# A feed-forward block in seven products: partial products run k block after k block, weight sums and gate rows moved

## The chip, the cores and the metric

The kernel runs on one core of a Trainium2 chip. The engines it uses are TensorE (PE: matmuls, with PEld for the load of their stationary operand), VectorE (DVE), ScalarE (ACT), GpSimd (POOL) and SyncE (SP, which issues the DMAs). The metric is the time of one execution in device microseconds; the median of three runs is given for the kernel before.

## The reference

One layer of a decoder: a mixing sub-layer (pooling and dilated attention heads) and a gated feed-forward block with a short convolution, each between norms and with a residual. 1024 tokens, a model width of 1024, an inner width of 2816. The change touches the feed-forward block and the end of the norm before it:

```
h  = rms_norm(x, g_pre_ffn) * (1.0 + sc_f) + sh_f
up = h @ w_up                                   # 1024 x (2 * 2816)
gate, val = up[..., :D_FF], up[..., D_FF:]
gate = conv over 3 tokens(gate) + conv_b
y  = (gelu(gate) * val) @ w_down
x  = x + gt_f * rms_norm(y, g_post_ffn)         # gt_f: a row of c_act @ w_ada + b_ada
```

## The kernel before

**Precision.** Every float32 factor is split in a high part, which TensorE takes in its rounded format, and a low part, the remainder. A product a x w is three partial products: high x high, high x low, low x high. ScalarE copies the high part, VectorE subtracts to get the low part. In the code the weights' parts are `wh`, `wl`, the activations' `ah`, `al` (or `gh`, `gl` in the down projection).

**Up projection.** It goes in 22 chunks `c` of 128 inner columns (gate and value together). Each chunk is a 2 x 2 block product done with seven block products instead of eight, numbered 1 to 7. The token halves of h and their sums are the moving operands (`a11`, `a12`, `a21`, `a22` and the sums `s1` to `s4`), the four weight blocks b11, b21, b12, b22 and their sums `t1` to `t4` the stationary ones; `USES` (L1049) says which product takes which. A product (`product`, L1058) has four k blocks of 128 and so twelve matmuls of 128 x 128 on 128 x 512, all into one bank of PSUM: per k block wh x ah (L1066), wh x al (L1067), wl x ah (L1068). From the second chunk on, GpSimd makes the sums t1 to t4 (`total`, L1135), ScalarE their high parts (`prep`, L1139) and VectorE their low parts (`lower`, L1132). VectorE also takes the finished banks (`evac`, L1072, and `first`, L1038) and runs the convolution.

**The order of the work.** TensorE, ScalarE, VectorE and GpSimd run in the order in which the program writes their instructions; nothing passes on one engine. `steps` (L1190) is the list of products from the second chunk on. At step i the weights of up to six later steps are prepared (`prep_up`, L1296), due tasks are run (`run_tasks`), and then the product is issued. SyncE's DMAs are issued in order on a queue of their own.

**The first chunk** (L983 to L1115, and L1303 to L1310) is written out by hand, between the end of the norm and the steady state. `stats` (L877) scales the tiles of tokens; the last tile (7) is scaled by VectorE at L899. It stands in the program ahead of the split of the fourth chunk's up-weights (`up_load(3)`, L985). The transposed tokens come back through ScalarE (L914); `sums` (L936) makes s1 to s4 for the second token half (VectorE, L941), `parts` splits them (ScalarE L122, VectorE L169), `start_sum` (L949) makes t1 to t4 of the first chunk (VectorE, L951). Order around product 7: s4's split, product 3, then sum s3, sum t3, split of t3, split of s3, product 7, the reading of products 6 and 5. Sum t4 stands later, at L1306, behind the split of b22 (L1304) and the reading of product 3. GpSimd's first t2 sum, for the second chunk, writes the tile that t4 reads, so it comes after t4.

**The gate row.** gt_f is made beside the up projection, in two halves of 512 columns: eight rows per half, one load each (SyncE, 256 KB, L1207) into one buffer, then one accumulation on VectorE (L1209, L1211). One row is done per step, from 14 steps before product (5, c) on, c being 16 for the first half and 19 for the second (L1254 to L1258); at product (5, c) one matmul sums over the partitions (`gate_sum`, L1215).

**Down projection.** Again seven products, in the order 1, 2, 6, 5, 3, 7, 4, each with eleven k blocks. Four token blocks t have a bank each. `down` (L1356) issues, for one k block and one t, gh x wh (L1361), gh x wl (L1362), gl x wh (L1363); the loop at L1409 goes over k and in it over t. With the last k block the sum of a bank is taken out (`out_sum`). In the last product the k blocks from 5 on are run t by t.

Of the kernel before, what the change touches and what calls it, by code (L numbers as in the profile page):

```python
# [15 lines left out]
P = 128  # L16
# [72 lines left out]
MLAG = (20, 48)  # L89
SPACE = 3  # L90
AHEAD = 3
GATE_AT = 16
SKIP = (0, 1, 4)
ENDS = 6
LAG_LO, LAG_EV = 1, 1
# [8 lines left out]
def block_kernel(ctx: ExitStack, tc: tile.TileContext, x, pos, cols, rows, consts, w_ada_a, w_ada_b, w_in_u,  # L104
# [764 lines left out]
    if True:  # L869
# [7 lines left out]
        def stats(ys, xs):  # L877
            n = len(ys) + len(xs)
            q = ep.tile([P, 4], F32, name="q1", tag="q1", bufs=3)
            yv = {}  # L880
            for i, t in enumerate(ys):
                d = st8[t]
                yv[t] = PS[:, y_bank(t):y_bank(t) + 2, :].rearrange("p a b -> p (a b)")
                d["xr"] = ep.tile([P, D], F32, name="xr", tag="xr", bufs=6)
                nc.sync.dma_start(d["xr"], xv[:, t])
                d["x1"] = ep.tile([P, D], F32, name="x1", tag="x1", bufs=4)
                junk = ep.tile([P, D], F32, name="junk", tag="junk")
                nc.scalar.activation(junk, yv[t], AF.Square, accum_out=q[:, i:i + 1])
            for i, t in enumerate(xs, len(ys)):
                junk = ep.tile([P, D], F32, name="junk", tag="junk")  # L890
                nc.scalar.activation(junk, st8[t]["x1"], AF.Square, accum_out=q[:, i:i + 1])
            r = rsqrt(q[:, 0:n], root(q[:, 0:n], n), n)
            for i, t in enumerate(ys):
                d = st8[t]
                nc.vector.scalar_tensor_tensor(d["x1"], yv[t], r[:, i:i + 1], gtg, op0=ALU.mult, op1=ALU.mult)
                nc.vector.tensor_add(d["x1"], d["x1"], d["xr"])
                nc.sync.dma_start(x1v[:, t], d["x1"])
            for i, t in enumerate(xs, len(ys)):
                nc.vector.tensor_scalar_mul(st8[t]["xr"], st8[t]["x1"], r[:, i:i + 1])  # L899

        def x_turn(m, r):
            for i in range(4):
# [24 lines left out]
        def side(name, k):  # L927
            for k0, h, l in reversed(A[name]):
                if k >= k0:
                    return h[:, k - k0], l[:, k - k0]  # L930
# [14 lines left out]
        def new_piece():  # L945
            at["p"] += 1
            return ring[(at["p"] - 1) % len(ring)]
# [5 lines left out]
        def start_piece(n, src):  # L953
            W[n, 0] = new_piece()
            split(src, *W[n, 0])
# [11 lines left out]
        if True:  # L967
# [90 lines left out]
            def product(n, c):  # L1058
                a, w = USES[n]
                wh, wl = W.pop((w, c))  # L1060
                used[n, c] = idle.pop(0)
                o = bank(used[n, c])
                for k in range(4):
                    ks = slice(k * P, (k + 1) * P)
                    ah, al = side(a, k)
                    nc.tensor.matmul(o, wh[:, ks], ah, start=k == 0, stop=False)  # L1066
                    nc.tensor.matmul(o, wh[:, ks], al, start=False, stop=False)  # L1067
                    nc.tensor.matmul(o, wl[:, ks], ah, start=False, stop=k == 3)  # L1068

            lo, hi = slice(0, 512), slice(512, 1024)  # L1070

# [25 lines left out]
            pairs_of("s4")  # L1097
            parts("s4", all_t)
            product(3, 0)
            sums(hi_t, (3,))  # L1100
            start_sum("t3", b12, b12, b22)
            more = r1.tile(half, F32R, name="more", tag="rb2")
            ring[:] = [(more[:, 2 * i], more[:, 2 * i + 1]) for i in range(2)]
            at["p"] = 0
            start_piece("t3", b12)
            pairs_of("s3")
            parts("s3", all_t)
            gelu = cp.tile([P, 1], F32, name="gelu")
            nc.scalar.activation(gelu, one, AF.Gelu_apprx_tanh)
            product(7, 0)  # L1110
            evac(6, 0)
            A["22"] = [(0, *(r2.tile(half, F32R, name="b22", tag=t) for t in ("r2a", "r2b")))]
            s1g = cp.tile([P, 512], F32, name="s1g", tag="cst")
# [5 lines left out]
    if True:  # L1119
# [131 lines left out]
            if n in (3, 4, 6, 7):  # L1251
                at_step(now[0] + LAG_EV, lambda: (evac(n, c), finish_4(c) if n == 4 else None))

        for hf, c in ((0, GATE_AT), (1, GATE_AT + 3)):  # L1254
            i = steps.index((5, c))
            EXTRA.setdefault(i, []).append(lambda hf=hf, c=c: gate_sum(hf, c))
            for kb in range(8):
                EXTRA.setdefault(i - 14 + kb, []).append(lambda hf=hf, kb=kb: gate_acc(hf, kb))  # L1258
        for c in range(1, NC_FF - 1):
            EXTRA.setdefault(START_AT[c] + 5, []).append(lambda c=c: at_step(now[0], lambda: first(c + 1)))  # L1260

# [41 lines left out]
        prep_up(5, 5)  # L1303
        parts("22", all_t)  # L1304
        evac(3, 0)
        start_sum("t4", b21, b21, t2r)  # L1306
        more = r1.tile([P, 8, 512], F32R, name="more", tag="rb0")
        ring += [(p1[:, 0], p1[:, 1])] + [(more[:, 2 * i], more[:, 2 * i + 1]) for i in range(4)]
        prep_up(6, 6)
# [30 lines left out]
    with tc.manual_schedule(engines={ET.PE}):  # L1340
# [12 lines left out]
        def dbank(n, t):  # L1353
            return bank(idle[4 * (DOWN.index(n) % 2) + t])

        def down(n, t, ks):  # L1356
            o = dbank(n, t)
            ts_ = slice(t * P, (t + 1) * P)
            for k in ks:
                (gh, gl), (wh, wl) = DW[n, k]  # L1360
                nc.tensor.matmul(o, gh[:, ts_], wh, start=k == 0, stop=False)  # L1361
                nc.tensor.matmul(o, gh[:, ts_], wl, start=False, stop=False)  # L1362
                nc.tensor.matmul(o, gl[:, ts_], wh, start=False, stop=k == KD - 1)  # L1363

        def y_half(T, hf, y, z=None):
            sl = slice(hf * 512, (hf + 1) * 512)
# [42 lines left out]
        for i, (n, k) in enumerate(dq):  # L1409
            while ready < i + AHEAD_D:  # L1410
                prep_down(ready)
                ready += 1
            if n == DOWN[-1] and k > KD - ENDS:
                continue
            ks = range(k, KD) if n == DOWN[-1] and k == KD - ENDS else (k,)
            for t in range(4):
                down(n, t, ks)
                if ks[-1] == KD - 1:
                    out_sum(n, t)


def _host(inputs):
# [56 lines left out]
```

## Time and profile before

| | |
|---|---|
| median of 3 runs | 1072.24 us (1071.94 to 1073.34) |
| the profiled execution's own time | 1068.81 us |
| its span, first to last instruction | 1067.0 us |
| mean granted TensorE clock | 0.993 |
| TensorE busy | 1034.3 us, 97% of the span |
| VectorE busy | 849.4 us, 80% |
| ScalarE busy | 479.4 us, 45% |
| GpSimd busy | 223.3 us, 21% |
| first chunk by hand, from product 5 on | 438 to 464 us of the span |
| up projection, products on TensorE | 438 to 850 us |
| down projection | 850 to 1060 us |

All times in the views count from the first instruction of the span. A row of a timeline has the start, the length, engine, line, operation, written tile <- read tiles, shape, count, and in brackets the idle time of the engine before it and what ended that. A row of waits has the total, the number and the longest. A row of stretches has its bounds, its length, and for each of PE, PEld, DVE, ACT and POOL the busy time and (x) the instructions, then the granted TensorE clock, the DMAs' busy share and GB/s. Grouped rows have the busy time and the mean in ns. A matmul's length in a row is modelled and overlaps the next one's; the distance of two starts is the better measure.

### The profile page before, as it was taken

The page shows a single profiled execution, that of the slowest core. Times are in us where ns is not written, and L with a number is a line of the kernel's source. Part 1 is how long each engine was busy: PE and PEld are TensorE (multiplying, and loading weights), DVE is VectorE, ACT ScalarE, POOL GpSimd, SP SyncE. Part 2 cuts the span into 40 slices and gives each one's busy share as a digit, 9 for nine tenths or more (in the row PEclk, how much of TensorE's full clock was granted, in tenths as well). Part 3 has the DMA queues.
Part 4 walks back from the last instruction along what each step waited for, and adds up shares of the span by engine and source line. Part 5 has one row for each costly group of instructions (what it writes and reads, how often), then busy time and mean ns, then how long its engine had stood idle before and what let it go on. Part 6 is the DMA issues. An engine that isn't in the chain of part 4 may idle for free.

```text
span 1067.0 us, 15433 instructions
## 1 busy us (share of the span) xinstructions
PE 1034.3 (97%) x5174; PEld 875.2 (82%) x5174; DVE 849.4 (80%) x1840; ACT 479.4 (45%) x963; POOL 223.3 (21%) x132
## 2 busy tenths in 40 slices
PE   4999999999999999899999999999999999999997
PEld 4988988899888788678888888888878878888885
DVE  7975467885558778989998987979789999756898
ACT  6764342433354378633443433333233365544542
POOL 0000000000000000064333333324235525103460
PEclk9999999999999999999999999999999999999999
DMA  9652446362131164224434333344534879566563
GB/s 350 226 158 79 118 110 199 93 189 79 52 95 49 50 237 151 97 91 146 147 129 162 126 123 135 134 161 151 162 115 155 294 274 380 168 195 209 200 207 119
DMA packets 85148, 168.34 MB, mean 158 GB/s; under 512 B 9158, under 2 KB 25926, under 8 KB 81356
## 3 DMA queue, kind: packets, MB, share of 16 engines
q1 hardware_dynamic: 85068, 167.35, 47.3%
q8 instruction: 41, 0.67, 0.3%
q14 instruction: 39, 0.32, 0.1%
HBM read 134.47 MB, written 32.84 MB: 157 GB/s over the span
## 4 chain that ended last, share of the span: by engine, by line
PE 67%; DVE 17%; DMA 6%; issue 4%; ACT 4%; SPq 0%; DVEq 0%; POOL 0%; ACTq 0%; POOLq 0%
PE PS L1068 7%; PE PS L1067 7%; PE PS L1066 7%; PE PS L1362 6%; PE PS L1361 6%; PE PS L1363 6%; PE PS L220 5%; PE PS L222 4%; PE PS L221 4%; DMA gm<-in_w_ada_b_dram 3%; PE PS L709 3%; PE PS L679 2%; DVE more L1133 2%; PE PS L699 1%; DMA mraw<-in_w_ada_b_dram 1%
## 5 line engine op out<-in xcount | busy, mean ns | idle before, releaser
L1137 POOL TENSOR_TENSOR raws<-rw 128x512 f32<-128x512 f32 x30 | 48.2, 1606 | 495.6 <-DMA rw<-in_w_up_dram 438.1
L220 PE MATMUL PS<-wh,hh 128*128 128x384 f32 x336 | 124.6, 371 | 0.8 <-DVE vs L269 0.7
L222 PE MATMUL PS<-wh,hl 128*128 128x384 f32 x336 | 113.2, 337 | 0.0
L221 PE MATMUL PS<-wl,hh 128*128 128x384 f32 x336 | 112.9, 336 | 0.0
L122 ACT ACTIVATE more<-raws 128x512 fp32r<-128x512 f32 x79 | 48.2, 624 | 74.0 <-PE PS L1067 57.1
L220 PEld LDWEIGHTS PS<-wh,hh 128*128 128x128 f32 x336 | 63.4, 189 | 9.1 <-issue 4.8
L688 ACT ACTIVATE pm<-pm,nm 128x128 f32<-128x128 f32 (+1 forms) x96 | 42.4, 443 | 62.9 <-DVE nm L686 43.4
L1133 DVE TENSOR_TENSOR more<-raws,more 128x512 fp32r<-128x512 f32 x74 | 67.1, 910 | 3.4 <-ACT more L122 3.4
L221 PEld LDWEIGHTS PS<-wl,hh 128*128 128x128 f32 x336 | 63.5, 189 | 0.6 <-issue 0.5
L222 PEld LDWEIGHTS PS<-wh,hl 128*128 128x128 f32 x336 | 63.1, 188 | 0.0
L1086 ACT ACTIVATE cv<-GG,col 128x1024 f32<-128x1024 f32 x22 | 27.4, 1246 | 71.4 <-DVE GG L1085 71.4
L682 DVE CUSTOM_DVE_ANT_0 pm<-PS,cst 128x128 f32<-128x128 f32 (+1 forms) x96 | 30.8, 347 | 30.5 <-PE PS L679 26.8
L1068 PE MATMUL PS<-a,more 128*128 128x512 f32 x136 | 53.2, 391 | 1.0 <-DVE more L1133 1.0
L1066 PE MATMUL PS<-a,more 128*128 128x512 f32 x136 | 52.9, 389 | 0.0
L1067 PE MATMUL PS<-a,more 128*128 128x512 f32 x136 | 52.9, 389 | 0.0
L1172 ACT ACTIVATE cv<-cv 128x1024 f32<-128x1024 f32 x22 | 23.4, 1062 | 62.1 <-DVE cv L1170 62.1
L1362 PE MATMUL PS<-tail 128*128 128x512 f32 x128 | 50.0, 391 | 0.4 <-DVE tail L169 0.4
L1361 PE MATMUL PS<-tail 128*128 128x512 f32 x128 | 49.8, 389 | 0.0
L1363 PE MATMUL PS<-tail 128*128 128x512 f32 x128 | 49.8, 389 | 0.0
L1137 POOL TENSOR_TENSOR t2r<-raws,rw 128x512 f32<-128x512 f32 x14 | 29.2, 2086 | 71.3 <-DVE more L1133 49.5
L1168 DVE SCALAR_TENSOR_TENSOR cv<-GG,col,cv 128x1023 f32<-128x1023 f32 x22 | 34.6, 1573 | 11.6 <-ACT cv L1086 11.6
L513 DVE SCALAR_TENSOR_TENSOR macc<-mraw,cact,macc 128x512 f32<-128x512 f32 x42 | 31.3, 745 | 12.4 <-DMA mraw<-in_w_ada_b_dram 12.4
(395 smaller groups left out, 3113.6 us busy)
## 6 DMA issues: line engine op xcount, KB each, us to landing
rw<-in_w_up_dram SPq DMA_DIRECT2D x21, 1024.0 KB
gscr<-VV SPq DMA_DIRECT2D x66, 256.0 KB
mraw<-in_w_ada_b_dram SPq DMA_DIRECT2D x48, 256.0 KB
R<-in_w_down_dram SPq DMA_DIRECT2D x48, 256.0 KB
raw<-in_w_in_u_dram SPq DMA_DIRECT2D x24, 384.0 KB
wa<-in_w_ada_a_dram SPq DMA_DIRECT2D x8, 1024.0 KB
R<-gscr SPq DMA_DIRECT2D x27, 256.0 KB
raws<-in_w_up_dram SPq DMA_DIRECT2D x25, 256.0 KB
```

The source lines that it names most:

```text
L122: nc.scalar.activation(o, i, AF.Copy)
L220: nc.tensor.matmul(o, a, wh[:, c0:c0 + 384], start=k == 0, stop=False)
L221: nc.tensor.matmul(o, a, wl[:, c0:c0 + 384], start=False, stop=False)
L222: nc.tensor.matmul(o, b, wh[:, c0:c0 + 384], start=False, stop=k == 7)
L1066: nc.tensor.matmul(o, wh[:, ks], ah, start=k == 0, stop=False)
L1067: nc.tensor.matmul(o, wh[:, ks], al, start=False, stop=False)
L1068: nc.tensor.matmul(o, wl[:, ks], ah, start=False, stop=k == 3)
L1133: nc.vector.tensor_tensor(wl, r, wh.bitcast(F32), ALU.subtract)
L1137: nc.gpsimd.tensor_tensor(t, a, b, ALU.add)
L1361: nc.tensor.matmul(o, gh[:, ts_], wh, start=k == 0, stop=False)
L1362: nc.tensor.matmul(o, gh[:, ts_], wl, start=False, stop=False)
L1363: nc.tensor.matmul(o, gl[:, ts_], wh, start=False, stop=k == KD - 1)
```

## The change

Five edits:

1. `product`: all four k blocks of one partial product, then the next partial product. In the first chunk (c = 0) the order is wh x ah, wl x ah, wh x al; in the later ones wh x ah, wh x al, wl x ah.
2. `down`: for each k block but the last, one partial product goes over all four token blocks (four banks), then the next. The last k block, and the last product's k blocks from 5 on, stay as they were.
3. The scaling of token tile 7 goes from VectorE to ScalarE.
4. In the first chunk, sum t3 and ScalarE's copy of its high part now stand ahead of sum s3, its low part behind; sum t4 stands right behind product 7, ahead of the reading of products 6 and 5.
5. The gate row: a row every second step, from 18 steps before the matmul on; the first half is summed at chunk 15 instead of 16, the second at 19 as before.

```diff
-GATE_AT = 16
+GATE_AT = 15
...
             for i, t in enumerate(xs, len(ys)):
-                nc.vector.tensor_scalar_mul(st8[t]["xr"], st8[t]["x1"], r[:, i:i + 1])
+                if t == NT - 1:
+                    nc.scalar.activation(st8[t]["xr"], st8[t]["x1"], AF.Copy, scale=r[:, i:i + 1])
+                else:
+                    nc.vector.tensor_scalar_mul(st8[t]["xr"], st8[t]["x1"], r[:, i:i + 1])
...
-                for k in range(4):
-                    ks = slice(k * P, (k + 1) * P)
-                    ah, al = side(a, k)
-                    nc.tensor.matmul(o, wh[:, ks], ah, start=k == 0, stop=False)
-                    nc.tensor.matmul(o, wh[:, ks], al, start=False, stop=False)
-                    nc.tensor.matmul(o, wl[:, ks], ah, start=False, stop=k == 3)
+                ws_, as_ = ((wh, 0), (wh, 1), (wl, 0)), []
+                for w_, low in ws_ if c else (ws_[0], ws_[2], ws_[1]):
+                    as_ += [(w_, low, k) for k in range(4)]
+                for i, (w_, low, k) in enumerate(as_):
+                    nc.tensor.matmul(o, w_[:, k * P:(k + 1) * P], side(a, k)[low], start=i == 0, stop=i == 11)
...
             product(3, 0)
-            sums(hi_t, (3,))
             start_sum("t3", b12, b12, b22)
...
-            start_piece("t3", b12)
+            W["t3", 0] = new_piece()
+            copy(nc.scalar, W["t3", 0][0], b12)
+            sums(hi_t, (3,))
+            nc.vector.tensor_tensor(W["t3", 0][1], b12, W["t3", 0][0].bitcast(F32), ALU.subtract)
             pairs_of("s3")
             parts("s3", all_t)
...
             product(7, 0)
+            start_sum("t4", b21, b21, t2r)
             evac(6, 0)
...
-        for hf, c in ((0, GATE_AT), (1, GATE_AT + 3)):
+        for hf, c in ((0, GATE_AT), (1, GATE_AT + 4)):
             i = steps.index((5, c))
             EXTRA.setdefault(i, []).append(lambda hf=hf, c=c: gate_sum(hf, c))
             for kb in range(8):
-                EXTRA.setdefault(i - 14 + kb, []).append(lambda hf=hf, kb=kb: gate_acc(hf, kb))
+                EXTRA.setdefault(i - 18 + 2 * kb, []).append(lambda hf=hf, kb=kb: gate_acc(hf, kb))
...
         evac(3, 0)
-        start_sum("t4", b21, b21, t2r)
...
-        def down(n, t, ks):
+        def down(n, t, ks, js=(0, 1, 2)):
             o = dbank(n, t)
             ts_ = slice(t * P, (t + 1) * P)
             for k in ks:
-                (gh, gl), (wh, wl) = DW[n, k]
-                nc.tensor.matmul(o, gh[:, ts_], wh, start=k == 0, stop=False)
-                nc.tensor.matmul(o, gh[:, ts_], wl, start=False, stop=False)
-                nc.tensor.matmul(o, gl[:, ts_], wh, start=False, stop=k == KD - 1)
+                for j in js:
+                    g, w = DW[n, k][0][j == 2], DW[n, k][1][j == 1]
+                    nc.tensor.matmul(o, g[:, ts_], w, start=k == 0 and j == 0, stop=k == KD - 1 and j == 2)
...
+            if ks[-1] < KD - 1:
+                for j in range(3):
+                    for t in range(4):
+                        down(n, t, ks, (j,))
+                continue
             for t in range(4):
                 down(n, t, ks)
-                if ks[-1] == KD - 1:
-                    out_sum(n, t)
+                out_sum(n, t)
```

## The prediction

> **What bounds the kernel now.** I read the page first, then TensorE's waits, then busy time by stretch, then the timelines of the stretches in which TensorE stands still.
>
> ```profile
> span 1067.0 us, 15433 instructions
> PE 1034.3 (97%) x5174; PEld 875.2 (82%) x5174; DVE 849.4 (80%) x1840; ACT 479.4 (45%) x963; POOL 223.3 (21%) x132
> PE PS L1066 <- ACT p L122: 2.0, 1, 2.0
> PE PS L1068 <- DVE more L1133: 1.0, 2, 0.6
> 480.65 0.39 PE L1066 MATMUL PS<-a,p 128*128 128x512 f32 x1
> 481.11 0.39 PE L1068 MATMUL PS<-a,p 128*128 128x512 f32 x1
> 483.37 0.39 PE L1066 MATMUL PS<-a,more 128*128 128x512 f32 x1
> 447.70:451.10 3.40, 1.55 (x6) 1.06 (x7) 3.02 (x4) 3.37 (x5) 0.00 (x0) 1.00 0.00 0
> 451.10:454.50 3.40, 3.40 (x10) 2.63 (x9) 2.86 (x5) 2.42 (x3) 0.00 (x0) 0.50 0.47 152
> 454.50:457.90 3.40, 2.65 (x12) 1.87 (x10) 2.54 (x3) 0.00 (x0) 0.69 (x1) 1.00 0.01 2
> 457.90:461.30 3.40, 1.70 (x6) 1.13 (x7) 2.13 (x3) 2.19 (x4) 3.40 (x3) 1.00 0.00 0
> 461.30:464.75 3.45, 3.45 (x9) 2.67 (x9) 3.45 (x4) 1.15 (x2) 3.37 (x3) 0.51 0.25 76
> ```
>
> TensorE (PE) is the bound, and almost everywhere a solid one: a product of twelve matmuls takes 483.37 - 480.65 = 2.72 us, 0.227 us each, and the step is the same where the weights change (from 480.65 to 481.11, the high part twice and then the low part, are two steps of 0.23). Only the places where it waits can be won: the first chunk (437 to 465), the gate rows (781 to 789) and the start of the down projection (866). In the first chunk the clock adds to it. The stretch before each 0.50 clock had TensorE busy for only 1.55 and 1.70 of 3.40 us; one with 2.65 was followed by a full clock. A half-clock stretch costs eight matmuls about 0.2 us each, 1.6 us.
>
> **The first chunk** hangs on VectorE (DVE), whose timeline names no idle time from 422.37 until 447; some of its rows, then ScalarE's, GpSimd's (POOL) and TensorE's:
>
> ```profile
> 421.66 1.04 ACT L122 ACTIVATE wh<-raw 128x1024 fp32r<-128x1024 f32 x1
> 53.64 1.05 ACT xt L324
> 422.37 0.16 DVE L161 SCALAR_TENSOR_TENSOR r<-v,r 128x1 f32<-128x1 f32 x1
> 422.56 0.75 DVE L899 TENSOR_SCALAR xr<-x,r 128x1024 f32<-128x1024 f32 x1
> 423.23 1.22 DVE L169 TENSOR_TENSOR wl<-raw,wh 128x1024 fp32r<-128x1024 f32 x1
> 424.37 1.22 DVE L941 TENSOR_TENSOR s1t<-raw_a,raw_b 128x1024 f32<-128x1024 f32 x1
> 445.25 1.21 DVE L941 TENSOR_TENSOR raw_b<-raw_a 128x1024 f32<-128x1024 f32 x1
> 448.77 2.36 DVE L169 TENSOR_TENSOR s3l<-raw_b,s3h 128x1024 fp32r<-128x1024 f32 x2 [0.25 <-ACT s3h L122]
> 453.55 2.29 DVE L169 TENSOR_TENSOR b<-raw_a,b 128x2048 fp32r<-128x2048 f32 x1 [0.50 <-ACT b L122]
> 456.36 0.69 DVE L951 TENSOR_TENSOR raws<-raws,t2r 128x512 f32<-128x512 f32 x1
> 459.17 1.11 DVE L1133 TENSOR_TENSOR p<-t2r,p 128x512 fp32r<-128x512 f32 x1 [2.13 <-ACT p L122]
> 457.21 1.26 POOL L1137 TENSOR_TENSOR t2r<-raws,rw 128x512 f32<-128x512 f32 x1 [21.77 <-DVE raws L951]
> 458.43 1.30 POOL L1137 TENSOR_TENSOR raws<-rw 128x512 f32<-128x512 f32 x1
> 438.16 0.50 PE L1066 MATMUL PS<-s,p 128*128 128x512 f32 x1 [0.30 <-ACT UU L122]
> 448.79 0.49 PE L1066 MATMUL PS<-s3h,more 128*128 128x512 f32 x1 [1.58 <-ACT s3h L122]
> 460.33 0.50 PE L1068 MATMUL PS<-s2h,p 128*128 128x512 f32 x1 [0.41 <-DVE p L1133]
> 463.93 0.63 PE L1066 MATMUL PS<-b,more 128*128 128x512 f32 x1
> ```
>
> *The row scaling moved to ScalarE.* It takes 0.67 us off VectorE (422.56 to 423.23), but it adds a wait on ScalarE (ACT): the scale r is ready at 422.53, and the nearest row for the operation is 1.05 us, so to 423.6. Behind it stands the copy of the fourth up-weight's high part (1.04, until now at 421.66): to 424.6. VectorE's next instruction is that weight's low part, which needs the copy, so its next one after that starts at about 425.8 instead of 424.37. VectorE is not 0.67 us earlier but **1.4 us later**, and nothing up to 447 takes it back. Bounds: 0.67 earlier, if the copy could pass, which one engine's order excludes; 1.4 later. I take 1.4.
>
> *First product.* It waits for a bank that ScalarE frees behind the s1 split: 438.16 + 1.4 = 439.6. The old second wait, for the low part of s1, is gone, since that is now wanted by the ninth matmul, not the second. It is over at 442.4.
>
> *Third sum, t3.* VectorE comes to it at 446.65. With t3's sum first, ScalarE's copy of t3 goes beside the s3 sum, and s3's high part is there at 449.6 (before 448.79); the second half lands at 450.5. TensorE waits 1.6 and 0.2 us. The low parts are wanted by the ninth matmul and no longer hold it.
>
> *Fourth sum, t4.* It is 0.69 us in front of five VectorE instructions. VectorE ends s3's low part at about 451.95 and t4 at 452.55, and POOL adds t2 at 452.7, not 457.21. But the wait moves: with POOL awake, VectorE's additions from memory queue behind POOL's. The row at 459.17 shows it: 1.11 us for a 0.68 us addition, which ended 0.55 after POOL's. So: two bank readings to 453.8; low part of t1 to 454.5; POOL's t3 to 455.7; the 2.2 us low part of b22 to 457.9; one bank reading to 458.5; POOL again to 459.1; t2's low part to **459.7**, against 460.28 now. If POOL takes its turn first at 453.9 it is 460.9.
>
> *TensorE at the end of it.* The product on t2 starts at about 456, runs eight matmuls and waits from 458.0 to 459.75 for t2's low part; four remain (0.34 after a wait, then 0.227), so the next product starts at about 460.8, against 463.93 now. If no half clock follows, the gain is 3.15 plus 0.4 us of half clock still running at 463.93: 3.55. If one follows, 1.6 less: **1.95**. Earlier half-clock stretches disappear into the waits. The last wait leaves TensorE busy about 1.65 of 3.40 us, nearest to the row with 1.70, which was followed by 0.50, so I take 1.95, with bounds 0.75 (POOL first) and 3.55.
>
> [...]
>
> **The gate rows.**
>
> ```profile
>   DMA gm<-in_w_ada_b_dram: 18.0, 12
> 784.21 0.75 DVE L1211 SCALAR_TENSOR_TENSOR gm<-gm,cact 128x512 f32<-128x512 f32 x1 [1.63 <-DMA gm<-in_w_ada_b_dram]
> 784.88 0.69 DVE L1133 TENSOR_TENSOR more<-raws,more 128x512 fp32r<-128x512 f32 x1
> 757.99 0.68 DVE L1133 TENSOR_TENSOR p<-rw,p 128x512 fp32r<-128x512 f32 x1
> 767.15 0.39 PE L1066 MATMUL PS<-s4h,p 128*128 128x512 f32 x1
> 782.03 0.50 PE L1068 MATMUL PS<-a,more 128*128 128x512 f32 x1 [0.39 <-DVE more L1133]
> 785.62 0.50 PE L1068 MATMUL PS<-a,more 128*128 128x512 f32 x1 [0.56 <-DVE more L1133]
> ```
>
> One buffer holds the row, so each load waits for the last accumulation, and VectorE stood 18.0 us behind twelve loads. The weights' low parts queue behind it; by 781 they are late, and three products lose 0.39, 0.56 and 0.47 us, each with some 0.3 of restart: 2.4 us. Two products apart, a row has 5.4 us for a load that takes about 2.6, so VectorE does not stand. The sixteen loads now block SyncE for two products instead of one, with the later up-weights' loads behind. Where no row has yet cost anything, a low part is ready at 758.67 for a product that starts at 767.15, so those loads have some 8 us of cover, and I cost the block at nothing (if that cover went, at most the 2.4 us would come back). The later low parts give 6 x 0.227 = 1.36 us more. Gain **2.4**; bounds 1.36 and 2.4.
>
> **Down.** At 866 the second matmul waits for a low part that POOL held up:
>
> ```profile
> 864.90 1.77 DVE L169 TENSOR_TENSOR tail<-raws,tail 128x512 fp32r<-128x512 f32 x1
> 866.73 0.50 PE L1362 MATMUL PS<-tail 128*128 128x512 f32 x1 [0.40 <-DVE tail L169]
> L409 PE MATMUL PS<-wl,hh 128*128 128x384 f32 x25 | 8.4, 335 | 0.0
> L405 PE MATMUL PS<-wh,hl 128*128 128x384 f32 x30 | 6.8, 335 | 0.0
> ```
>
> It is now wanted by the fifth matmul, 0.68 us later: the wait (0.40, with restart 0.67) goes. Gain **0.7**, bounds 0 and 0.7. The new order changes the bank with every matmul, 780 of them. L405 does that, L409 does not, and both take 335 ns: no cost.
>
> **The sum.** 1.95 + 2.4 + 0.7 = 5.05. The profiled execution took 1068.81 us (span 1067.0, 1.8 around it); it would be 1063.8. The median of the runs shown is 1072.24, 3.4 above the profiled one; the difference is taken from there: **1067.2 us**.
>
> **Rivals.**
> 1. No half clock after the last wait (25%): 3.55 + 2.4 + 0.7 = 6.65, 1065.6. For it: 1.75 us can fall across two stretches of the clock. Against: the 1.70 row.
> 2. VectorE is not delayed by the row scaling (15%): t2's low part 1.4 us earlier, that wait short and no half clock: 3.55 + 1.4 + 3.1 = 8.05, 1064.2. Against: the order on ScalarE.
> 3. The first chunk only moves its wait (17%): POOL first, and a half clock that no wait hides: 0.75 - 1.6 + 1.36 + 0 = 0.5, or up to 1.9 with the gate rows and down partly won: about 1070.8, within 0.2% (2.1 us, about what a measurement of this kernel can tell from no change). The change would then do what it says without being worth it.
> 4. Slower (3%): changing banks with each matmul makes TensorE pause in the down projection until its clock drops. It costs 1.6 us a half-clock stretch; from the fourth it eats the 5.05, from five on it is slower by more than 0.2%: six give 1072.24 - 5.05 + 9.6 = 1076.8. Against: L405. [...]
>
> The forecast has 40%. The range takes in rivals 1 and 2 and most of 3: **1063.3 to 1070.5**. Faster by over 0.2%: 40 + 25 + 15 and a little of the third, 0.84; same 0.13; slower 0.03.
>
> **What would show it.** On VectorE an idle of about 2 us ahead of the low part at 423, released by ScalarE, and the s1t sum at 425.8: if it starts before 424.4, the first step is wrong. The first product at 439.6; s3's at 449.6; no wait of POOL's t2 until 457; t2's low part near 459.7, with POOL's additions between. TensorE's wait for it stands before the ninth matmul of that product; whether 0.50 stands in the clock behind it decides between forecast and rival 1. No wait of VectorE for gate rows above a few tenths, none of TensorE between 470 and 850. In the down projection 0.227 us a matmul. A time above 1070.1 or a matmul step above 0.227 would make the prediction wrong.

## The result, and the profile after

| | before | after |
|---|---|---|
| median of 7 runs | 1072.31 us (1069.79 to 1073.34) | 1065.12 us (1063.39 to 1070.46) |
| the profiled execution | 1068.81 us | 1066.22 us |

The ratio of the times is 0.994 (95%: 0.9921 to 0.996), that is 4.3 to 8.5 us less. The forecast was 1067.2 us, with a range of 1063.3 to 1070.5, and faster as the likeliest sign; the measured time lies inside. Most of its steps held; two that did not cancelled each other. Two executions, one of the kernel before at a mean granted clock of 0.656 (1468.66 us) and the only profiled one of xr_back (experiment 1) at 0.736 (1320.11 us), are left out of every comparison.

The top of the page of the kernel after:

```profile
span 1064.4 us, 15419 instructions
PE 1034.1 (97%) x5174; PEld 875.2 (82%) x5174; DVE 854.2 (80%) x1839; ACT 487.4 (46%) x964; POOL 218.3 (21%) x132
```

Its waits, TensorE's and VectorE's for the gate rows (total us, number, longest us):

```profile
PE PS L1070 <- ACT UU L122: 1.8, 1, 1.8
PE PS L1070 <- DVE p L1138: 1.5, 1, 1.5
PE PS L1070 <- DVE VV L1080: 1.4, 1, 1.4
DVE gm L1216 <- DMA gm<-in_w_ada_b_dram: 3.8, 2, 1.9
```

TensorE is busy as long as before. The waits that the forecast wanted gone are gone (the 2.0 for ScalarE's copy of t2's high part, the low parts behind the gate rows, 18.0 us of VectorE behind twelve loads down to 3.8 behind two), and one is there that it did not have: 1.4 us for VV, a bank that VectorE has to read. The 3.8 us of VectorE were not forecast either, but no wait of TensorE follows from them.

**A common zero.** The program up to the end of the norm is the same in both, yet this execution came to it 2.4 us later, so two spans cannot simply be subtracted. All that follows counts from one small ScalarE instruction, the square root in the norm of tile 7, which is called the root here. Before:

```profile
421.45 0.30 ACT L151 ACTIVATE sd<-q,epst 128x1 f32<-128x1 f32 x1
...
849.59 0.39 PE L1361 MATMUL PS<-tail 128*128 128x512 f32 x1
```

From the root to the end of the span the kernel before took 1067.0 - 421.45 = 645.6 us. The timeline of the kernel after, ScalarE, VectorE, GpSimd, then TensorE:

```profile
423.84 0.30 ACT L151 ACTIVATE sd<-q,epst 128x1 f32<-128x1 f32 x1
424.94 1.15 ACT L900 ACTIVATE xr<-x,r 128x1024 f32<-128x1024 f32 x1 [0.81 <-DVE r L161]
426.00 1.04 ACT L122 ACTIVATE wh<-raw 128x1024 fp32r<-128x1024 f32 x1
427.08 1.23 DVE L169 TENSOR_TENSOR wl<-raw,wh 128x1024 fp32r<-128x1024 f32 x1 [2.17 <-ACT wh L122]
428.22 1.22 DVE L944 TENSOR_TENSOR s1t<-raw_a,raw_b 128x1024 f32<-128x1024 f32 x1
454.39 0.69 DVE L954 TENSOR_TENSOR raws<-raws,t2r 128x512 f32<-128x512 f32 x1
455.24 1.29 POOL L1142 TENSOR_TENSOR t2r<-raws,rw 128x512 f32<-128x512 f32 x1 [15.95 <-DVE raws L954]
457.00 3.41 DVE L169 TENSOR_TENSOR b<-raw_a,b 128x2048 fp32r<-128x2048 f32 x1
460.94 1.16 DVE L1138 TENSOR_TENSOR p<-t2r,p 128x512 fp32r<-128x512 f32 x1
442.01 4.59 PE L1070 MATMUL PS<-s,p 128*128 128x512 f32 x12 [1.77 <-ACT UU L122]
462.15 1.20 PE L1070 MATMUL PS<-s2h,p 128*128 128x512 f32 x4 [1.52 <-DVE p L1138]
463.19 1.08 PE L1070 MATMUL PS<-b,more 128*128 128x512 f32 x4
847.90 5.60 PE L1366 MATMUL PS<-tail 128*128 128x512 f32 x24
```

Here the root to the end is 1064.4 - 423.84 = 640.6 us: **5.0 us less**, beside a predicted sum of 5.05. With 423.84 - 421.45 = 2.39 taken off, the rows stand beside the forecast like this:

| step | predicted | measured, on the clock of before |
|---|---|---|
| sum s1t starts on VectorE | 425.8 | 425.83 |
| first product | 439.6 | 439.62 |
| t4 on VectorE | 451.95 | 452.00 |
| GpSimd's t2 | 452.7 | 452.85 |
| t2's low part done | 459.7 | 459.71 |
| the next product | 460.8 | 460.80 |

**Where the 5.0 us came from.** Three landmarks: the first product `a,p` of the steady state that both traces name (480.65 before; 481.52 after, below), the first matmul of the down projection, the end. Up to the first landmark 59.20 against 57.68, a gain of 1.52. From there to the down projection 368.94 against 366.38, a gain of 2.56. From there to the end 217.4 against 216.5, a gain of 0.9. The forecast had 1.95, 2.4 and 0.7. But the 1.52 is not the 1.95 a little smaller: it is a gain of about 3.5 and a loss of 2.0. The product behind the one on t2 starts 463.93 - 421.45 = 42.48 us behind the root before and 463.19 - 423.84 = 39.35 after, 3.1 earlier, and 0.4 us of half clock that still ran there before is gone. From there to the landmark the kernel before took 480.65 - 463.93 = 16.72 us, that 0.4 included, and the kernel after 481.52 - 463.19 = 18.33; the six products between need 72 x 0.227 = 16.3.

That the gain is 3.5 and not 1.95 comes from the clock. Stretches of the trace after (length, busy us of PE, PEld, DVE, ACT and POOL, granted clock, DMA share, GB/s):

```profile
439.73:443.14 3.41, 1.64 (x8) 1.02 (x7) 3.38 (x4) 2.73 (x5) 0.00 (x0) 1.00 0.00 0
443.14:446.56 3.42, 3.42 (x10) 2.64 (x9) 3.42 (x6) 2.86 (x4) 0.00 (x0) 0.50 0.00 0
...
460.21:463.62 3.41, 1.89 (x8) 1.24 (x7) 3.41 (x6) 2.01 (x4) 3.33 (x3) 1.00 0.00 0
463.62:467.03 3.41, 3.41 (x16) 2.76 (x15) 3.41 (x3) 1.96 (x4) 3.13 (x2) 1.00 0.29 84
```

The wait for t2's low part was 1.52 us, not 1.75, and TensorE was busy for 1.89 us of its stretch. The clock stayed at 1.00. The half clock after the first product's wait (busy 1.64) cost nothing at the end: that product took 4.4 us where the forecast has 2.8 (439.6 to 442.4; the next one starts at 446.39), but the wait for s3's high part behind it shrank from 1.58 us to a single one of 0.2.

The 2.0 went here. VectorE's reading of the bank before, then after, with the tap ahead of it, and TensorE's timeline after:

```profile
476.46 0.67 DVE L1078 TENSOR_TENSOR VV<-VV,PS 128x512 f32<-128x512 f32 x1
...
475.57 2.19 DVE L1175 SCALAR_TENSOR_TENSOR cv<-GG,col,cv 128x1022 f32<-128x1022 f32 x1
477.69 0.68 DVE L1080 TENSOR_TENSOR VV<-VV,PS 128x512 f32<-128x512 f32 x1
478.51 1.17 PE L1070 MATMUL PS<-s2h,more 128*128 128x512 f32 x4 [1.41 <-DVE VV L1080]
481.52 2.98 PE L1070 MATMUL PS<-a,p 128*128 128x512 f32 x12
```

TensorE wants a bank of PSUM. VectorE has still to read it (L1080, product 3 of the second chunk), and its reading stands behind the convolution of the first chunk, L1173 and L1175. TensorE is more than 3 us earlier, but this reading is only 1.2 us earlier (55.0 us behind the root before, 53.85 after), so that a reading that was in time before came 1.41 us late.

### The profile page after: what moved, and what is told of

Same layout as the page of the kernel before. It is cut to its first block, busy times and chain, and to the rows that moved or that the text cites. A ratio compares the mean times of both kernels' runs of the same rounds, so it can differ in the third digit from the quotient of the medians.

```text
span 1064.4 us, 15419 instructions
## 1 busy us (share of the span) xinstructions
PE 1034.1 (97%) x5174; PEld 875.2 (82%) x5174; DVE 854.2 (80%) x1839; ACT 487.4 (46%) x964; POOL 218.3 (21%) x132
## 4 chain that ended last, share of the span: by engine, by line
PE 84%; DVE 8%; ACT 3%; DMA 3%; issue 2%; SPq 0%; DVEq 0%; ACTq 0%
PE PS L1070 35%; PE PS L1366 20%; PE PS L220 5%; PE PS L222 5%; PE PS L221 4%; PE PS L709 3%; PE PS L679 2%; PE PS L699 2%; DVE acc L342 1%; PE PS L594 1%; PE PS L596 1%; PE PS L595 1%; DMA mraw<-in_w_ada_b_dram 1%; PE PS L620 1%; DVE more L1138 1%
## 5 line engine op out<-in xcount | busy, mean ns | idle before, releaser
L1070 PE MATMUL PS<-a,more 128*128 128x512 f32 x408 | 95.4, 389 | 0.0
L1366 PE MATMUL PS<-tail 128*128 128x512 f32 x384 | 91.4, 389 | 0.0
L1070 PEld LDWEIGHTS PS<-a,more 128*128 128x128 f32 x408 | 76.6, 188 | 15.9
L1366 PEld LDWEIGHTS PS<-tail 128*128 128x128 f32 x384 | 72.1, 188 | 14.9
L688 ACT ACTIVATE pm<-pm,nm 128x128 f32<-128x128 f32 (+1 forms) x96 | 42.4, 443 | 64.7 <-DVE nm L686 41.4
L1366 PE MATMUL PS<-more 128*128 128x512 f32 x300 | 70.1, 389 | 0.0
L1366 PEld LDWEIGHTS PS<-more 128*128 128x128 f32 x300 | 56.3, 188 | 11.7
L1070 PE MATMUL PS<-s,more 128*128 128x512 f32 x252 | 61.5, 393 | 0.1
L1070 PE MATMUL PS<-b,more 128*128 128x512 f32 x252 | 60.6, 389 | 0.0
L1070 PEld LDWEIGHTS PS<-s,more 128*128 128x128 f32 x252 | 47.2, 188 | 11.2 <-issue 1.5
L1070 PEld LDWEIGHTS PS<-b,more 128*128 128x128 f32 x252 | 47.3, 188 | 9.9
L1177 ACT ACTIVATE cv<-cv 128x1024 f32<-128x1024 f32 x22 | 23.4, 1062 | 66.4 <-DVE cv L1175 66.4
```

Of the source, the lines that this page charges most:

```text
L688: nc.scalar.activation(pm[:, h, 0:nk * P], pm[:, h, 0:nk * P], AF.Exp, bias=nm[:, h:h + 1], scale=0.125, accum_out=U[:, h, HD + 1:HD + 2])
L1070: nc.tensor.matmul(o, w_[:, k * P:(k + 1) * P], side(a, k)[low], start=i == 0, stop=i == 11)
L1177: nc.scalar.activation(cv, cv, AF.Gelu_apprx_tanh)
L1366: nc.tensor.matmul(o, g[:, ts_], w, start=k == 0 and j == 0, stop=k == KD - 1 and j == 2)
```

## The experiments

All counts "from the root" are the span's end less the start of the root in the same trace, as above (before 645.6, after 640.6). This takes away what happened ahead of the change, mostly spells of half clock (24.43 to 27.84 us before, 180.32 to 187.14 after); a half clock behind the root is still in it.

| kernel | root to end, us | median, us | ratio to before (95%) |
|---|---|---|---|
| xr_back_2 | 638.97 | 1064.69 | 0.993 (0.9912 to 0.9949) |
| copy_first | 638.34 | 1063.34 | 0.9917 (0.9898 to 0.9935) |
| order_only | 646.5 | 1070.36 | 0.9991 (0.9973 to 1.0009) |
| prod_order_back | 640.54 | 1066.08 | 0.9933 (0.9912 to 0.9953) |
| down_back | 641.5 | 1066.45 | 0.9932 (0.9909 to 0.9955) |
| gate_back | 644.8 | 1069.33 | 0.9982 (0.9967 to 0.9997) |
| t3t4_back | 646.05 | 1068.81 | 0.997 (0.9957 to 0.9982) |
| taps_later | 637.75 | 1061.10 | 0.9898 (0.9878 to 0.9918) |
| b22_later | 637.66 | 1062.19 | 0.9915 (0.9897 to 0.9933) |

Beside the interval of the kernel after (0.9921 to 0.996), those of gate_back and order_only lie clear above it and that of taps_later clear below, and t3t4_back's just touches it; what is read from the other kernels rests on one trace of each. How far one trace carries is seen where the edits change nothing: from `a,p` to the down projection the kernel after, xr_back_2, copy_first, prod_order_back, down_back and t3t4_back take 366.28 to 366.40 us. The down projection is less even: 216.50 to 216.84 us in five kernels without a wait of TensorE there, up to 218.53 with small waits whose cause stays open (experiment 5).

**1. The row scaling back on VectorE (xr_back, and again as xr_back_2).**

```diff
-                if t == NT - 1:
-                    nc.scalar.activation(st8[t]["xr"], st8[t]["x1"], AF.Copy, scale=r[:, i:i + 1])
-                else:
-                    nc.vector.tensor_scalar_mul(st8[t]["xr"], st8[t]["x1"], r[:, i:i + 1])
+                nc.vector.tensor_scalar_mul(st8[t]["xr"], st8[t]["x1"], r[:, i:i + 1])
```

> The changed kernel with the row scaling of token tile 7 back on VectorE; all else stays. All times here are counted from ScalarE's root of tile 7 (L151, one column), since the program ahead of it is the same in all kernels; from there to the end of the span it was 1067.0 - 421.45 = 645.6 us before and 1064.4 - 423.84 = 640.6 us after the change, and the low part of t2 on VectorE ended at 38.8 and 38.3 us. Theory: VectorE's order in the first chunk sets the pace, and the moved row costs 1.4 us. VectorE's idle of 2.2 us ahead of the low part of the fourth up-weight goes, the first s1t sum starts at 2.9 us instead of 4.4, t2's low part ends at about 36.9 us, and the end comes at 639.2 us, the median 1.4 us below that of the changed kernel. Rival: later waits of TensorE (the bank of product 6 of chunk 2) absorb it; then the s1t sum is earlier, but the end stays at 640.6 us. Second rival: the row is worth its move, and without it VectorE's 0.67 us come back: the end is later than 640.6 us.

The five other executions of xr_back have a median of 1064.74 us. The kernel was profiled again:

> Once more the changed kernel with the row scaling of tile 7 back on VectorE, since the first profile of it was taken at a clock of 0.74. From tile 7's root to the end it was 640.6 us in the changed kernel and 638.4 with the copy first. Theory (VectorE's order in the first chunk sets the pace): the first s1t sum at 2.9 us from the root, t2's low part done at 36.9 us, the end at 639.2 us. Rival, for which the first medians speak (1065.19 here, 1065.12 for the changed kernel): the s1t sum is earlier, but the end stays at 640.6 us.

The timeline of xr_back_2, ScalarE, VectorE, TensorE:

```profile
425.13 0.30 ACT L151 ACTIVATE sd<-q,epst 128x1 f32<-128x1 f32 x1
428.04 1.22 DVE L941 TENSOR_TENSOR s1t<-raw_a,raw_b 128x1024 f32<-128x1024 f32 x1
460.74 1.19 DVE L1135 TENSOR_TENSOR p<-t2r,p 128x512 fp32r<-128x512 f32 x1
461.99 1.20 PE L1067 MATMUL PS<-s2h,p 128*128 128x512 f32 x4 [0.37 <-DVE p L1135]
```

Sum s1t starts 2.91 us behind the root, against 4.38 in the kernel after, and t2's low part is done 36.80 behind it, against 38.26. TensorE's wait for it falls from 1.52 to 0.37 us, and the end comes 1.6 us earlier. So edit 3, the move to ScalarE, is a loss of about 1.5 us inside a change that gains 5. The medians (1064.69 and 1065.12) are too close to show it by themselves.

**2. The scaling on ScalarE, but behind the copy that VectorE waits for (copy_first).**

```diff
                 if t == NT - 1:
+                    up_load(AHEAD)
                     nc.scalar.activation(st8[t]["xr"], st8[t]["x1"], AF.Copy, scale=r[:, i:i + 1])
...
-                if c + 2 <= AHEAD:
+                if c + 2 < AHEAD:
```

> The changed kernel with the split of the fourth up-weight written ahead of ScalarE's row scaling of tile 7, so that ScalarE copies that weight's high part while VectorE still works on the scale. Theory: VectorE goes on 0.2 us after the scale, its first s1t sum starts about 1.9 us earlier than in the changed kernel (at 2.4 us from tile 7's root instead of 4.4), t2's low part ends near 36.3 us, and the end comes at about 638.7 us from the root; the median is 1.9 us below that of the changed kernel. The transposes that need the scaled row start 2.9 us after the root; the row is ready at 2.3 us, so they do not wait. Rival: the time does not follow VectorE's order here; then the end stays at 640.6 us.

ScalarE's and VectorE's timeline in copy_first:

```profile
423.54 0.29 ACT L151 ACTIVATE sd<-q,epst 128x1 f32<-128x1 f32 x1
423.74 1.04 ACT L122 ACTIVATE wh<-raw 128x1024 fp32r<-128x1024 f32 x1
424.69 1.14 ACT L901 ACTIVATE xr<-x,r 128x1024 f32<-128x1024 f32 x1
425.96 1.22 DVE L945 TENSOR_TENSOR s1t<-raw_a,raw_b 128x1024 f32<-128x1024 f32 x1
```

Now s1t starts 2.42 behind the root, ahead of either kernel, and the root to end is 638.34 (638.7 was expected). So the edit is no loss once it stands behind that copy; against xr_back_2 it is 0.5 us ahead on VectorE and 0.6 at the end, by one trace each. The wait for VV stays at 1.3 us, since all of VectorE and TensorE moved together.

**3. The new order of the partial products alone (order_only):** the kernel before with edits 1 and 2 and none of the others.

```diff
+                ws_, as_ = ((wh, 0), (wh, 1), (wl, 0)), []
+                for w_, low in ws_ if c else (ws_[0], ws_[2], ws_[1]):
+                    as_ += [(w_, low, k) for k in range(4)]
...
+            if ks[-1] < KD - 1:
+                for j in range(3):
+                    for t in range(4):
+                        down(n, t, ks, (j,))
+                continue
```

> The kernel before with the new order of the partial products alone, in the up and in the down projection; the row scaling, the first chunk's sums and the gate rows stay as before. Theory: the order moves only when a low part is wanted. In the first chunk the waits for the low parts of s1 and s3 and the second wait on t2 go (0.6, 0.8 and 0.4 us), those for a bank, for s3's high part (1.6) and for t2's high part (2.0) stay. At the gate rows the three low parts come later and later (0.55, 0.73 and 0.63 us lost one after the other, 1.9 in all), of which 1.36 is covered, so about 0.5 us stays. The wait in the down projection goes (0.7). From tile 7's root to the end 645.6 - 1.5 - 1.9 - 0.7 = 641.5 us where the half clock stays as it was, up to 3.2 less without it. Rival: the order does all of it, and the end is at 640.6 us or below with the clock as before. Second rival: it does nothing, 645.6 us.

The gate rows in TensorE's timeline:

```profile
789.48 1.20 PE L1067 MATMUL PS<-s4h,p 128*128 128x512 f32 x4 [0.54 <-DVE p L1132]
798.08 3.00 PE L1067 MATMUL PS<-b,more 128*128 128x512 f32 x12 [1.04 <-DVE UU L1074]
```

646.5 us from the root, 0.9 more than before and not the 641.5 of the theory, and a ratio whose interval holds 1: alone, the edit in the headline shows no gain (the interval leaves room for at most 2.9 us). The waits tell why. In the first chunk the small waits for low parts are gone, but the one for s3's high part has grown from 1.58 to 2.3 us and the one for ScalarE's copy of t2's high part from 2.04 to 2.6. At the gate rows TensorE starts its products sooner, and then stands 1.04 us for a bank that the same late VectorE has not read.

**4. The old order of the up products in the kernel after (prod_order_back):** edit 1 undone, the k-by-k loop of before put back.

> The changed kernel with the up projection's products in the old order (k block by k block, three matmuls each); the down projection keeps its new order, and so do the other edits. Theory: with VectorE as the bound of the first chunk the order hardly matters by itself. Low parts are wanted 1.36 us sooner, so the product on t2 is over 1.36 us later, but the wait for the bank of product 6 of chunk 2 (1.4 us) shrinks by the same amount; the old second waits for the low parts of s1 and s3 (0.6 and 0.8 us) come back but lie ahead of the wait for t2 and so shorten that. Nothing at the gate rows, where the low parts are now early. From tile 7's root to the end 640.6 to 641.0 us with the clock as in the changed kernel. Rival, as the prediction had it: the order is worth its 1.36 us per late low part, and the end is at 642 us or later.

TensorE's waits in it:

```profile
PE PS L1071 <- DVE p L1139: 2.0, 1, 2.0
...
PE PS L1071 <- DVE more L1139: 0.5, 1, 0.5
PE PS L1070 <- DVE s3l L169: 0.5, 1, 0.5
```

and VectorE's reading of the bank, with the root at 425.00:

```profile
478.77 0.68 DVE L1081 TENSOR_TENSOR VV<-VV,PS 128x512 f32<-128x512 f32 x1
```

The waits for low parts come back, 0.3 to 0.5 us each, and t2's grows from 1.5 to 2.0. But VectorE reads the bank 53.8 us behind the root in both kernels, TensorE comes to it later, and of the wait of 1.41 a pause of 0.10 is left. The root to end is 640.54, the same as after. What the order lets TensorE have early it gives back at the next bank.

**5. The old order in the down projection (down_back).**

```diff
             if ks[-1] < KD - 1:
-                for j in range(3):
-                    for t in range(4):
-                        down(n, t, ks, (j,))
+                for t in range(4):
+                    down(n, t, ks)
                 continue
```

> The changed kernel with the down projection's matmuls in the old order (token block by token block). Theory, as in the prediction: the low part that came 0.7 us late at its first blocks is late again, and from tile 7's root to the end it is 641.3 us. Rival: VectorE, no longer held up by the gate rows, reaches the down projection early enough in either order; then it stays at 640.6 us. Against a third possibility, that changing the bank with every matmul costs time, stands the step of 0.227 us in both.

The timeline of TensorE near the end:

```profile
1041.68 0.96 PE L1366 MATMUL PS<-tail 128*128 128x512 f32 x3 [0.23 <-DVE tail L169]
```

The wait at the start of the down projection, 0.40 us in the kernel before, does not come back: with the old order there is no TensorE wait between 860 and 1040. So the order was not what removed it. The 0.9 us that this kernel is longer are two waits of 0.23 and 0.24 us near 1042 with their restarts. Waits like these stand there in order_only, t3t4_back and taps_later too, which have the new order, and not in the kernel before, which has the old; what decides them stays open.

**6. The old gate rows in the kernel after (gate_back).**

```diff
-GATE_AT = 15
+GATE_AT = 16
...
-        for hf, c in ((0, GATE_AT), (1, GATE_AT + 4)):
+        for hf, c in ((0, GATE_AT), (1, GATE_AT + 3)):
...
-                EXTRA.setdefault(i - 18 + 2 * kb, []).append(lambda hf=hf, kb=kb: gate_acc(hf, kb))
+                EXTRA.setdefault(i - 14 + kb, []).append(lambda hf=hf, kb=kb: gate_acc(hf, kb))
```

> The changed kernel with the gate rows as before (a row every step, the first half summed at chunk 16). Theory, after the run with the order alone: the order of the partial products only puts the lateness off. VectorE still stands behind the row loads, the low parts get later from product to product, and then the banks are freed late as well; TensorE loses about 3.0 us between 780 and 800 (0.3, 0.6 and 0.8 before low parts, 1.3 before a bank), and from tile 7's root to the end it is 643.6 us. Rival, as in the prediction: the later low parts cover 1.36 us and about 0.5 us stays; then 641.1 us. Second rival: the order covers all of it, 640.6 us.

Every wait of TensorE between 780 and 1062 us:

```profile
784.19 3.02 PE L1070 MATMUL PS<-a,more 128*128 128x512 f32 x12 [0.60 <-DVE more L1138]
787.65 1.21 PE L1070 MATMUL PS<-a,more 128*128 128x512 f32 x4 [0.44 <-DVE more L1138]
791.17 1.20 PE L1070 MATMUL PS<-s4h,p 128*128 128x512 f32 x4 [0.47 <-DVE p L1138]
799.76 2.98 PE L1070 MATMUL PS<-b,more 128*128 128x512 f32 x12 [1.05 <-DVE UU L1077]
869.22 2.12 PE L1366 MATMUL PS<-tail 128*128 128x512 f32 x8 [0.29 <-DVE tail L169]
```

VectorE stands 19.0 us behind twelve loads again. 644.8 us: the gate rows are worth 4.2 us in this kernel, the largest single term beside experiment 7's. The three low-part waits are back in spite of the new order, the bank wait of 1.05 is the one of order_only, and the one at 869 shows that the down projection's wait comes with the old gate rows, 80 us earlier. VectorE's lateness is the likely way: between 800 and 850 us it is busy for 47.5 of 50 us in the kernel before, with the same gate rows, and for 41.4 in the kernel after. No run shows that by itself.

**7. Sums t3 and t4 back in their old places (t3t4_back):** edit 4 undone (`sums(hi_t, (3,))` ahead of `start_sum("t3", ...)`, `start_sum("t4", b21, b21, t2r)` behind the reading of product 3).

> The changed kernel with the sums t3 and t4 of the first chunk at their old places. Theory: GpSimd's t2 waits for sum t4 again, so that VectorE stands about 2 us before t2's low part, which ends near 40.2 us from tile 7's root instead of 38.3; TensorE's product on t2 is over about 2.6 us later, its later wait for a bank comes about 1.9 us later, and the end is at about 642.5 us (640.6 in the changed kernel), with up to 3.2 us more for half clocks. Rival: VectorE makes it up, since GpSimd then no longer holds up the low part of b22; the end stays within 0.5 us of 640.6 us.

GpSimd's and TensorE's timeline:

```profile
460.71 1.26 POOL L1139 TENSOR_TENSOR t2r<-raws,rw 128x512 f32<-128x512 f32 x1 [21.78 <-DVE raws L954]
462.69 2.08 PE L1070 MATMUL PS<-s2h,p 128*128 128x512 f32 x4 [4.17 <-ACT p L122]
```

The chain of before is back: GpSimd waits for t4 to be out of its tile, 37.25 us behind the root instead of 31.4, TensorE stands 4.17 us for the high part of t2, and the matmuls behind it start 0.43 us apart (eight from 464.56 to 467.97), as they did at half clock before (six from 451.48 to 454.04). 646.05, so edit 4 is worth 5.5 us by this trace. Of that 2.0 lie in the down projection, with four small waits between 1046 and 1050 of the kind that experiment 5 leaves open; 3.5 lie ahead of `a,p` (61.23 us behind the root against 57.68) and are the edit's own, the half clock included. The waits that edits 4 and 5 remove are not independent of one another (a later TensorE asks less of VectorE), so the terms need not add up to 5.0.

**8. The convolution of the first chunk later (taps_later):** copy_first with the taps of chunk 0 moved one and a half steps behind, past the reading of product 3. In this kernel the convolution of chunk 0 reads gate values in its first token half that chunk 2 has already written over, so that part of the output is another one; the instructions and their lengths are the same.

```diff
-            at_step(i + 1, lambda: taps(c, g))
-            at_step(i + 2, lambda: gated(c, v))
+            d = 1.5 if c == 0 else 0
+            at_step(i + 1 + d, lambda: taps(c, g))
+            at_step(i + 2 + d, lambda: gated(c, v))
```

> The kernel of the run with the copy first, and in it the convolution of chunk 0 on VectorE (two taps, and the product with the value behind it) moved behind the reading of products 3 and 7 of chunk 1. Theory: TensorE's new wait of 1.4 us in the changed kernel, ahead of product 6 of chunk 2, is for the bank that VectorE frees only behind those two taps; it goes, together with its restart, and the end comes about 1.6 us earlier than with the copy first alone, at about 637.1 us from tile 7's root. Rival: VectorE as a whole is behind, the wait turns up at the next bank or weight, and the end stays at 638.7 us.

VectorE's timeline:

```profile
469.64 0.67 DVE L1081 TENSOR_TENSOR VV<-VV,PS 128x512 f32<-128x512 f32 x1
473.96 1.27 DVE L1174 SCALAR_TENSOR_TENSOR cv<-GG,col,cv 128x1023 f32<-128x1023 f32 x1
```

The reading now stands ahead of the taps, and TensorE has no wait for VV at all. So that was the cause of the new wait. Up to `a,p` the whole of it is won, 1.7 us: 53.72 us behind the root, against 55.41 in copy_first. At the end only 0.6 of it is left (638.34 to 637.75). 0.5 is lost ahead of the down projection, where TensorE waits 0.32 us for another bank at 505.61, and 0.6 in the down projection, with a small wait at 1039.31. So the rival is right in part.

**9. The reading earlier, ahead of the taps (b22_later):** copy_first, with the reading of product 3 of chunk 1 half a step earlier and the convolution of chunk 0 0.6 of a step later, so that the reading stands ahead of the taps, and the 2 us split of b22 behind the split of t2 instead of ahead of it.

```diff
-            at_step(i + 1, lambda: taps(c, g))
-            at_step(i + 2, lambda: gated(c, v))
+            d = 0.6 if c == 0 else 0
+            at_step(i + 1 + d, lambda: taps(c, g))
+            at_step(i + 2 + d, lambda: gated(c, v))
...
-                at_step(now[0] + LAG_EV, lambda: (evac(n, c), finish_4(c) if n == 4 else None))
+                at_step(now[0] + LAG_EV - 0.5 * ((n, c) == (3, 1)), lambda: (evac(n, c), finish_4(c) if n == 4 else None))
...
         prep_up(5, 5)
+        evac(3, 0)
+        ring.append((p1[:, 0], p1[:, 1]))
+        prep_up(6, 6)
         parts("22", all_t)
-        evac(3, 0)
         more = r1.tile([P, 8, 512], F32R, name="more", tag="rb0")
-        ring += [(p1[:, 0], p1[:, 1])] + [(more[:, 2 * i], more[:, 2 * i + 1]) for i in range(4)]
-        prep_up(6, 6)
+        ring += [(more[:, 2 * i], more[:, 2 * i + 1]) for i in range(4)]
```

> The kernel with the copy first, and two more moves: product 3 of chunk 1 is read from its bank ahead of the two taps of chunk 0, and the split of b22 (VectorE 2.3 us, 3.4 us where GpSimd holds it up) stands behind the split of t2 for chunk 1. The product that needs b22 comes only after the one that needs t2. Theory: TensorE's wait for t2's low part (1.56 us and its restart with the copy first) and the one for the bank (1.29 and its restart) both go, and from tile 7's root to the end it is about 638.4 - 1.6 - 1.5 = 635.3 us; what stays is the wait for s3's high part (1.9 us). Rival: VectorE is the bound of this stretch as a whole, the waits turn up at the next banks, and the end is at 637 us or later.

VectorE's timeline:

```profile
452.55 1.21 DVE L1139 TENSOR_TENSOR p<-t2r,p 128x512 fp32r<-128x512 f32 x1
453.98 3.10 DVE L169 TENSOR_TENSOR b<-raw_a,b 128x2048 fp32r<-128x2048 f32 x1 [0.22 <-ACT b L122]
```

t2's low part is done 32.9 us behind the root, 3.3 earlier than in copy_first. TensorE's waits for it and for VV are gone, and the one for s3's high part, 1.9 us, is what is left of the chain. The time, 637.66, lies on the rival's side of the expectation. The waits did not turn up again as the rival has it; but the wait for s3 is now followed by a half clock (0.60 on average from 447.80 to 451.20) with no wait behind it to hide it, about 1.6 us by the prediction's price. The median of 1062.19 us is 10 us below before and 3 below after; against the kernel after, the intervals of the two ratios still overlap (0.9897 to 0.9933, and 0.9921 to 0.996).

## Why the prediction was right, and where it was wrong

- **Row scaling, VectorE 1.4 us later: right** to 0.03 us, and with it the cause: copy_first takes away the order on ScalarE, and the delay goes. Rival 2 is out with it.
- **First product, t3 and t4: right.** GpSimd's t2 and the product after moved as worked out, t2's low part to within 0.01 us of 459.7. GpSimd's and VectorE's additions did hold each other up (1.16 us for t2's low part, and 3.41 instead of 2.29 us for b22's).
- **The half clock behind the last wait: wrong.** This was the term "1.6 less: 1.95", taken because 1.65 us of busy time was nearest to the row with 1.70. Busy was 1.89 and the clock stayed whole, as rival 1 has it, so this part of the first chunk gave 3.5. Rival 1's reason, a wait across two stretches of the clock, no run shows. What was measured is the wait, 460.63 to 462.15: TensorE came to it 0.2 us later than worked out, so that it was 1.52 us and not 1.75.
- **"None of TensorE between 470 and 850": wrong.** This is the step that failed. The forecast worked out the slack of a weight's low part at the gate rows, and none for the banks that VectorE must read when TensorE comes earlier. One came 1.41 us late, and with restart and a small pause at 481 it cost 2.0. The two errors, +1.6 and -2.0, nearly cancel; that the sum came out at 5.05 against 5.0 is luck in this part.
- **Gate rows, 2.4: right in the difference of the traces (2.56), wrong in the bounds.** 1.36 was to be the lower bound because the new order covers late low parts. gate_back shows the cover is worth nothing: the lateness comes back as a bank wait of 1.05 us, and the edit is worth 4.2 there. The sign "no wait of VectorE for gate rows above a few tenths" failed: before the last row of each half it stands 1.92 and 1.89 us (704.75 and 781.78). It cost nothing, as TensorE waits nowhere between 482 and 1062 us; that the row loads in SyncE's queue cost nothing was right too.
- **Down projection, 0.7: the size about right (0.9), the cause wrong.** It was put down to the order of the partial products. With the new gate rows neither order waits there; with the old ones the kernel before waits 0.40, gate_back 0.29 with the new order, and order_only not at all. The new gate rows are what removes it, probably through VectorE; that the order helps a late VectorE now and then is not excluded.
- **No price for changing banks with each matmul: right.** Rival 4 did not happen; no run here shows TensorE pausing at a change of bank. TensorE's timeline of the kernel after:

```profile
861.50 5.60 PE L1366 MATMUL PS<-tail 128*128 128x512 f32 x24
866.94 2.88 PE L1366 MATMUL PS<-tail,p 128*128 128x512 f32 x12
```

Here 24 matmuls take 866.94 - 861.50 = 5.44 us, 0.227 each, as before. By median the change is worth 7.2 us and by the root 5.0; the interval of the ratio (4.3 to 8.5) holds both, and the difference is not explained by anything that the change does.

## What to carry to other kernels

When TensorE comes earlier at one place, go through everything that the slower in-order engine owes it over the next chunk: not only the operands it makes, but also the banks it has to empty. An order of matmuls that wants an operand later did not help here against an engine that is late, since the same engine holds the next bank (1.05 us of wait in gate_back); move the work that makes it late. And before an instruction is moved to an engine with time to spare, look at what stands behind it in that engine's queue, and who waits for that.

## What the runs showed of the hardware that was not expected

- **The clock.** In the first chunk the kernel before has two stretches at half clock and the kernel after has one, each 3.41 to 3.42 us long (451.10 to 454.51 and 461.33 to 464.75; 443.14 to 446.56). In the 3.4 us ahead of them TensorE was busy for 1.55, 1.70 and 1.64 us; behind 2.65 us (454.50, before) and 1.89 us (460.21, after) the clock stayed at 1.00. Busy time alone does not tell what follows: from 176.91 to 180.32 the kernel after was also busy for 1.89 us, in other matmuls (128x1 and 64x256 among them), and there the clock stood at 0.50 from 180.32 to 187.14. Nor does the length of a wait. gate_back waits 1.80 us for its first product, and the twelve matmuls behind that wait start 0.24 us apart (442.13 to 444.98); prod_order_back waits 1.78 us there, and from 445.26 to 448.67 its matmuls start 0.43 us apart. Later it waits 1.99 us for t2's low part, and the matmuls behind go on at 0.23 us. For s3's high part b22_later and copy_first both wait 1.68 us; the clock was 0.60 on average from 447.80 to 451.20 in the one and 1.00 from 450.20 to 453.60 in the other. What decides it these runs do not show.
- **GpSimd and VectorE.** With GpSimd adding, VectorE's subtraction for b22 took 3.41 us instead of 2.29, and the tap at 475.57 took 2.19 where the same row in b22_later, with no GpSimd work beside it, took 1.28: this is part of why the bank is read so late. GpSimd's sum at 458.23 took 3.32 us beside the b22 subtraction, where the same sum took 1.75 before (459.68).
